# The order of row tiles in the down pairs of a two-layer decoder trunk, and the place of a bias table's product

## The chip, the cores and the metric

The kernel runs on one core of a Trainium2 chip. The metric is the time of one execution in microseconds on the device. Below, TensorE is the matrix engine (PE in the profile), VectorE is DVE, ScalarE is ACT, GpSimd is POOL and SyncE is SP. SyncE only issues transfers here.

## The reference, cut to what matters

The reference is a decoder trunk of two layers for 256 tokens of width 2048. Each layer has a mixer (layer 0: retention and forgetting attention; layer 1: differential attention and a sparse attention with a bias table), a SwiGLU block, and an embedding stage that is gated by the residual stream. The change touches the last matrix product of the SwiGLU block, and, in the embedding stage of layer 0, one small product for the bias table of layer 1.

```python
for i in range(DEPTH):
    ...                                              # mixer: x = x + mix
    h = rmsnorm(x, norm_ffn[i])
    x = x + (jax.nn.silu(h @ ffn_gate[i]) * (h @ ffn_up[i])) @ ffn_down[i]
    x = x + jax.nn.sigmoid(x @ ple_gate[i]) * (p[i] @ ple_proj[i])
return rmsnorm(x, final_norm)
```

The hidden width is 5632. In layer 1 the attention logits get a bias `table[t5_bucket(distance)]` from `t5_table` (32 buckets, 16 heads).

## The kernel before, in words

**Products.** All tokens stand as two halves of 128 rows. An fp32 product is made of three matmuls: each operand is split into a high part (a rounded copy, made by ScalarE) and a low part (the rest, made by VectorE), and high x high, high x low and low x high are summed. A *row tile* is 256 rows by 512 columns of a weight matrix. It is loaded by SyncE into one of five `raw` buffers, split into `whi` and `wlo` (L197, L199), and multiplied with both halves of the tokens: 2 x 2 x 3 = 12 matmuls of 512 columns (L352, L353, L355) into a pair of PSUM accumulators `acc`. There are four of these accumulators, two for each of two blocks of 512 output columns.

**Pairs.** Two blocks of columns, a and b, are computed together as a *pair* (`pair`). For the first 512 rows of the weights the pair uses a scheme of seven products in place of eight, of 6 matmuls each (`Quad`, L421 to L423). They have numbers: 1, 2, 3 and 7 take a weight tile from memory, 5, 6 and 4 take sums of such tiles, which VectorE makes in place (`add`, L385: two sums for product 7, one for 6, one for 4). Sums of the activations (`tabs`) serve as the other operand. After 6 and 5 VectorE combines results in z tiles. The rest of the rows go as plain row tiles, a or b. A string gives the order in which the steps of a pair are taken: a digit is a product, a letter the next row tile of that block. Product 4 completes block a: behind it VectorE adds the parts to both accumulators (`close`, L441, L442) and runs the block's evacuation. Block b is closed and evacuated behind its last row tile.

**The order of issue.** All steps of the program stand in one list, and the kernel is written out by a loop over it (`run`). At each step the splits of weights are issued up to three steps ahead (`LOOK`), then the step's matmuls. Then one tick of `background` passes: small generators (turning a tile, softmax, tables) each issue their next piece when the number of ticks they yielded has passed. Engines work in order, so what is issued first stands first. A weight load is issued when one of the five buffers is free; the tiles of products have their own buffers (`e`, three, and `keys`), and SyncE's queue is in the order of the steps.

**The SwiGLU block.** The 11 blocks of hidden columns are made in three parts: 0 to 3, 4 to 7 and 8 to 10 (here parts 1, 2 and 3; p = 0, 1, 2 in the code). In each part, gate and up of a hidden block form one pair; then the part's hidden blocks are multiplied with `ffn_down` in two pairs, columns 0 and 1, then 2 and 3 (c = 0 and c = 2). A down pair of parts 1 and 2 has 8 row tiles for each block, two of which go into the seven products: 19 steps. One of part 3 has 6, so 15 steps. The last two row tiles of a block read the part's last hidden block, which has just been made: `evac_up` writes it (L1163), and `hid_steps` turns it by way of memory (`turn_far`: two VectorE transposes, L540; one transfer out, L542; four back, L545) and, seven ticks later, splits it into the operand (`split_far`, L498 on ScalarE and L499 on VectorE; the tiles are called Ah, Al or Bh, Bl). Hidden block 10 is turned on TensorE instead (L512). Evacuation of a down block adds it to x (`add_x`, L612); in part 3 it also starts the turn of x for the embedding stage, one column block after the other.

**The embedding stage.** Four row tiles of `ple_proj` come first, one for each block of 512 columns, evacuated by L1195 and L1196, then 32 row tiles of `ple_gate`. At its beginning in layer 0 the generator `toep_steps` starts: it loads the bias table and a one-hot matrix `ohr` by GpSimd (L1028, L1030), yields, multiplies them on TensorE (L1033, a product of 384 columns), copies the result (L1035), writes it to memory spread over 32 rows (L1038) and reads it back in four transfers (L1042) as the table that the attention of layer 1 uses.

Of the kernel before, what the change touches and what calls it, by code (L numbers as in the profile page):

```python
# [95 lines left out]
class Kernel:  # L96
# [344 lines left out]
            tt(blk.acc[0], blk.acc[0], first, op=OP.add)  # L441
            tt(blk.acc[1], blk.acc[1], second, op=op)  # L442

    def pair(self, names, layer, keys, c0, nch, stat, k0, sums, evacs, needs, **kw):

        a, b = (self.Block(self, stat, evac, k0=k0, **{n: v[i] for n, v in kw.items()}) for i, evac in enumerate(evacs))
        q = a.quad = b.quad = self.Quad(self, a, b, stat, k0 + 2 * c0, sums)
        key = {p: (names[i], layer, (keys[i], c0 + c)) for p, i, c in ((1, 0, 0), (2, 0, 1), (3, 1, 1), (7, 1, 0))}
        rest = [(c, c == c0 + nch - 1) for c in range(c0 + 2, c0 + nch)]

        def quad(p):
            self.prog.append(("quad", key.get(p), q, p, needs(c0)))

        def mm(i, c, last):
            self.mm(names[i], layer, (keys[i], c), (a, b)[i], last, needs(c))

        a_rest, b_rest = list(rest), list(rest)
        for what in "1a3a7a6a2aab5b4bbbb" if len(rest) == 6 else "1a3a7a62ab5b4bb":
            if what == "a":
                mm(0, *a_rest.pop(0))  # L460
            elif what == "b":
                mm(1, *b_rest.pop(0))
            else:
                quad(int(what))
# [557 lines left out]
    def toep_steps(self):  # L1022

        nc = self.nc
        self.toep = self.const.tile([P, 16, S], F32, name="tabs")
        tab = self.sc.tile([33, 16], F32, name="tab", bufs=1)
        nc.vector.memset(tab[32:33, :], NEG)
        nc.gpsimd.dma_start(tab[:32, :], self.io["t5_table"])  # L1028
        ohr = self.ring.tile([33, 384], F32, name="z", bufs=8)
        nc.gpsimd.dma_start(ohr, self.io["ohr"])  # L1030
        yield "at", 2
        at = self.ps.tile([P, 512], F32, name="at", bufs=2)
        nc.tensor.matmul(at[:16, :384], tab, ohr, start=True, stop=True)  # L1033
        vec = self.ring.tile([16, 384], F32, name="z", bufs=8)
        nc.scalar.activation(vec, at[:16, :384], AF.Copy)  # L1035

        dv = self.dram.tile([16, 32, 384], F32, name="dv")
        nc.gpsimd.dma_start(dv, vec[:, None].to_broadcast([16, 32, 384]))  # L1038
        yield None, 3
        for q in range(4):  # L1040
            src = bass.AP(tensor=dv.tensor, offset=dv.offset + P - 1 - 32 * q, ap=[[383, 32], [32 * 384, 16], [1, S]])
            nc.gpsimd.dma_start(self.toep[32 * q:32 * q + 32], src)  # L1042
            if q < 3:
                yield None, 1
# [89 lines left out]
    def ffn(self, layer, src, mid, tag, tag2):  # L1134
        K, nc = self, self.nc
        hs = {}

        def evac_gate(blk):
            K.need([("norm", 3)])
            sg = K.zt()  # L1140
            for h in range(2):
                nc.scalar.activation(sg[:, h], blk.acc[h], AF.Silu, scale=K.rstd[:, h:h + 1])
            if blk.j == 10:
                K.table("sigmoid_and_others")
            hs[blk.j] = sg

        def hid_steps(j, k0, hid):
            if j == 10:
                yield from K.turn_fast(hid, mid, k0)
                return  # L1150
            t = K.turn_far(hid)
            yield None, 7
            K.split_far(t, mid, k0)
            if k0 == 0:
                yield None, 1
                for _ in K.sums_of(lambda k, h: K.far(t)[:, k:k + 2, h], K.sums[:, 1]):
                    yield None, 1

        def evac_up(blk):
            sg = hs.pop(blk.j)  # L1160
            hid = K.zt()
            for h in range(2):
                nc.vector.scalar_tensor_tensor(hid[:, h], blk.acc[h], K.rstd[:, h:h + 1], sg[:, h],  # L1163
                                               op0=OP.mult, op1=OP.mult)
            K.spawn(("hid", layer, blk.j), hid_steps(blk.j, (blk.j - blk.j0) * 4, hid),
                    kind="tp" if blk.j == 10 else None)

        def evac_down(blk):
            K.add_x(blk)
            if blk.lastpart:  # L1170
                K.after_x(blk.cb, tag2, src, None, squares=False)

        for p, (j0, j1) in enumerate(FFN_PARTS):
            for j in range(j0, j1):
                if j == 0:
                    self.blocks("ffn_gate", layer, j, 8, src, evac_gate, j=j,
                                needs=[[(tag, c // 2)] for c in range(8)])
                    self.blocks("ffn_up", layer, j, 8, src, evac_up, j=j, j0=j0)
                else:
                    self.pair(("ffn_gate", "ffn_up"), layer, (j, j), 0, 8, src, 0, lambda: K.sums[:, 0],  # L1180
                              (evac_gate, evac_up), lambda c: [("sums", tag)], j=(j, j), j0=(j0, j0))
            for c in range(0, 4, 2):
                if p == 2:
                    self.prog.append(("call", (lambda: K.load_p(layer)) if c == 0 else K.split_p))
                hid = lambda j: [("hid", layer, j // 2)]
                self.pair(("ffn_down", "ffn_down"), layer, (c, c + 1), 2 * j0, 2 * (j1 - j0), mid, -4 * j0,
                          lambda: K.sums[:, 1], (evac_down, evac_down), hid, cb=(c, c + 1), lastpart=(p == 2,) * 2)

    def ple(self, layer, src, tag, tag2, dst, gain):
# [246 lines left out]
```

## Time and profile before

| | us |
|---|---|
| median of 3 runs | 2520.8 |
| lowest and highest run | 2516.07, 2525.46 |
| the profiled execution | 2528.45 |
| its span, from the first to the last instruction | 2526.7 |
| TensorE busy | 2475.3 (98%) |
| VectorE busy | 1860.0 (74%) |
| ScalarE busy | 1291.6 (51%) |
| mean granted clock of TensorE | 0.991 |

Busy time is the union of an engine's instructions in that one execution. The ends of matmuls are modelled: a matmul of 512 columns is shown as 0.39 us, while the next begins 0.23 us after it. A granted clock of 1.00 is TensorE's full speed. Idle time in brackets is that of the engine ahead of the instruction, with what ended it.

### The profile page before, as it was taken

Reading aid. Unit: us, or ns where it says so; the run is one execution under the profiler, and the core shown is the slowest. Engines: PE = TensorE matmul, PEld = TensorE weight load, DVE = VectorE, ACT = ScalarE, POOL = GpSimd, SP = SyncE. Lnnn points to the kernel's source line nnn. Section 1 sums busy time; section 2 is a strip of 40 time slices with the busy share of each in tenths; the row PEclk is TensorE's granted clock in tenths of the full one; section 3 lists DMA queues with packets and bytes.
Section 4 is the critical chain, followed back from the end, with each engine's and each line's share of the span. In section 5 each row is a group of like instructions: output and inputs, shape, how many; then the busy total and the mean of one; then the engine's idle time right before and its main releaser. Section 6 shows DMA issues by size and latency. Waiting matters only on the chain.

```text
span 2526.7 us, 30918 instructions
## 1 busy us (share of the span) xinstructions
PE 2475.3 (98%) x11284; PEld 2034.3 (81%) x11284; DVE 1860.0 (74%) x2427; ACT 1291.6 (51%) x1701; POOL 140.7 (6%) x261
## 2 busy tenths in 40 slices
PE   8999999999999999998999999999999999999998
PEld 7888888787788878776889888878778887888777
DVE  5867756688788887887654666657878888788975
ACT  5444445555445554554553555555544555455554
POOL 0000001000000000101010000010000000000000
PEclk9999999999999999999999999999999999999999
DMA  7655557676556666657857344576665666657564
GB/s 271 188 175 175 184 176 237 205 234 201 189 195 221 224 200 216 206 209 198 254 176 243 129 129 160 172 223 234 200 215 191 208 225 209 215 185 241 176 223 138
DMA packets 146537, 508.70 MB, mean 201 GB/s; under 512 B 18037, under 2 KB 18549, under 8 KB 146256
## 3 DMA queue, kind: packets, MB, share of 16 engines
q1 hardware_dynamic: 132560, 464.25, 55.2%
q0 software_dynamic: 13392, 41.85, 6.1%
q8 instruction: 88, 1.44, 0.2%
q14 instruction: 65, 0.53, 0.1%
q10 hardware_dynamic: 432, 0.62, 0.1%
HBM read 485.42 MB, written 21.23 MB: 201 GB/s over the span
## 4 chain that ended last, share of the span: by engine, by line
PE 77%; DVE 9%; issue 7%; DMA 4%; ACT 2%; POOL 1%; SPq 0%; DVEq 0%; ACTq 0%; POOLq 0%
PE acc L353 22%; PE acc L355 22%; PE acc L352 22%; DVE wlo L199 2%; DVE wlo L182 1%; PE at L422 1%; PE at L421 1%; PE at L423 1%; DMA z<-far 1%; DVE e L385 1%; PE acc L421 1%; PE acc L422 1%; PE acc L423 1%; DMA far<-z 1%; DVE z L1163 1%
## 5 line engine op out<-in xcount | busy, mean ns | idle before, releaser
L199 DVE TENSOR_TENSOR wlo<-raw,whi 128x1024 fp32r<-128x1024 f32 (+3 forms) x753 | 896.6, 1192 | 439.1 <-ACT whi L197 436.9
L197 ACT ACTIVATE whi<-raw 128x1024 fp32r<-128x1024 f32 (+3 forms) x753 | 776.9, 1034 | 554.9 <-PE acc L355 480.3
L352 PE MATMUL acc<-whi,Ah 128*128 128x512 f32 (+1 forms) x1536 | 603.1, 393 | 12.2 <-ACT whi L197 7.3
L353 PE MATMUL acc<-wlo,Ah 128*128 128x512 f32 (+1 forms) x1536 | 598.7, 390 | 5.5 <-DVE wlo L199 4.1
L355 PE MATMUL acc<-whi,Al 128*128 128x512 f32 (+1 forms) x1536 | 596.8, 389 | 2.4 <-DVE Al L499 1.5
L352 PE MATMUL acc<-whi,Bh 128*128 128x512 f32 (+2 forms) x1440 | 560.9, 390 | 4.3 <-ACT Bh L498 4.3
L353 PE MATMUL acc<-wlo,Bh 128*128 128x512 f32 (+2 forms) x1440 | 555.6, 386 | 4.2 <-DVE wlo L199 3.1
L355 PE MATMUL acc<-whi,Bl 128*128 128x512 f32 (+2 forms) x1440 | 554.7, 385 | 1.6 <-DVE Bl L499 1.6
L353 PEld LDWEIGHTS acc<-wlo,Ah 128*128 128x128 f32 x1536 | 291.0, 189 | 73.1 <-DVE wlo L199 16.6
L352 PEld LDWEIGHTS acc<-whi,Ah 128*128 128x128 f32 x1536 | 290.9, 189 | 72.5 <-ACT whi L197 7.3
L355 PEld LDWEIGHTS acc<-whi,Al 128*128 128x128 f32 x1536 | 291.1, 190 | 63.9 <-DVE Al L499 2.9
L353 PEld LDWEIGHTS acc<-wlo,Bh 128*128 128x128 f32 x1440 | 272.3, 189 | 64.9 <-DVE wlo L199 13.9
L352 PEld LDWEIGHTS acc<-whi,Bh 128*128 128x128 f32 x1440 | 271.9, 189 | 57.0 <-ACT Bh L498 5.4
L355 PEld LDWEIGHTS acc<-whi,Bl 128*128 128x128 f32 x1440 | 272.0, 189 | 56.7 <-DVE Bl L499 2.9
L180 ACT ACTIVATE whi<-e 128x1024 fp32r<-128x1024 f32 x160 | 169.7, 1061 | 229.2 <-DVE e L385 154.8
L182 DVE TENSOR_TENSOR wlo<-e,whi 128x1024 fp32r<-128x1024 f32 x160 | 194.6, 1216 | 49.0 <-ACT whi L180 44.9
L385 DVE TENSOR_TENSOR e<-e 128x1024 f32<-128x1024 f32 x96 | 116.9, 1218 | 1.1
L542 POOL DMA_DIRECT2D far<-z x35 | 27.0, 771 | 1446.3 <-DVE z L540 1446.3
L180 ACT ACTIVATE whi<-keys 128x1024 fp32r<-128x1024 f32 x64 | 67.6, 1056 | 54.6 <-DVE keys L385 31.4
L182 DVE TENSOR_TENSOR wlo<-keys,whi 128x1024 fp32r<-128x1024 f32 x64 | 78.3, 1224 | 22.5 <-ACT whi L180 20.9
L545 POOL DMA_DIRECT2D z<-far x140 | 76.6, 554 | 137.9 <-DMA far<-z 59.3
L721 ACT ACTIVATE e<-e,m 128x128 f32<-128x128 f32 (+2 forms) x96 | 40.1, 419 | 75.5 <-DVE m L719 75.5
(298 smaller groups left out, 2186.8 us busy)
## 6 DMA issues: line engine op xcount, KB each, us to landing
raw<-in_ffn_gate SPq DMA_DIRECT2D x136, 512.0 KB, 3.8
raw<-in_ffn_up SPq DMA_DIRECT2D x136, 512.0 KB, 3.5
raw<-in_ffn_down SPq DMA_DIRECT2D x128, 512.0 KB, 3.7
raw<-in_w_in_even SPq DMA_DIRECT2D x103, 512.0 KB, 4.2
raw<-in_w_in_odd SPq DMA_DIRECT2D x80, 512.0 KB, 4.0
raw<-in_ple_gate SPq DMA_DIRECT2D x56, 512.0 KB, 4.5
e<-in_ffn_up SPq DMA_DIRECT2D x40, 512.0 KB, 4.5
e<-in_ffn_down SPq DMA_DIRECT2D x36, 512.0 KB, 4.5
```

Of the source, the lines that this page charges most:

```text
L180: nc.scalar.activation(hi, r, AF.Copy)
L182: nc.vector.tensor_tensor(lo, r, hi.bitcast(F32), op=OP.subtract)
L197: nc.scalar.activation(hi[:, c], r[:, c], AF.Copy)
L199: nc.vector.tensor_tensor(lo[:, c], r[:, c], hi[:, c].bitcast(F32), op=OP.subtract)
L352: nc.tensor.matmul(o, sh, wh, start=not self.started[h], stop=False)
L353: nc.tensor.matmul(o, sh, wl, start=False, stop=False)
L355: nc.tensor.matmul(o, sl, wh, start=False, stop=end)
L385: r, add = self.raw, lambda o, x: self.K.nc.vector.tensor_tensor(o, o, x, op=OP.add)
L421: nc.tensor.matmul(o, sh[:, i], wh, start=start and i == 0, stop=False)
L422: nc.tensor.matmul(o, sh[:, i], wl, start=False, stop=False)
L423: nc.tensor.matmul(o, sl[:, i], wh, start=False, stop=i == 1 and p in (1, 4, 5, 6, 7))
L545: nc.gpsimd.dma_start(back[32 * c:32 * c + 32].rearrange("p (q f) -> p q f", q=4), far[c].rearrange("(q i) f -> i q f", q=4))
```

## The change

Three things change. `pair` takes the order of its steps as an argument, and gate and up get the order that they had. The down pairs get an order for each part and pair:

| part, pair | before | after |
|---|---|---|
| 1 and 2, first | 1a3a7a6a2aab5b4bbbb | 1a3a7a6a2b5bbbaa4bb |
| 1 and 2, second | 1a3a7a6a2aab5b4bbbb | the same |
| 3, first | 1a3a7a62ab5b4bb | 1a3a7b6b2a5a4bb |
| 3, second | 1a3a7a62ab5b4bb | 1a3a7a62a5b4bbb |

And `toep_steps` yields 8 ticks in place of 2 between its two loads and its product. No operation is added or removed.

```diff
-    def pair(self, names, layer, keys, c0, nch, stat, k0, sums, evacs, needs, **kw):
+    def pair(self, plan, names, layer, keys, c0, nch, stat, k0, sums, evacs, needs, **kw):
...
-        for what in "1a3a7a6a2aab5b4bbbb" if len(rest) == 6 else "1a3a7a62ab5b4bb":
+        for what in plan:
...
-        yield "at", 2
+        yield "at", 8
         at = self.ps.tile([P, 512], F32, name="at", bufs=2)
         nc.tensor.matmul(at[:16, :384], tab, ohr, start=True, stop=True)
...
-                    self.pair(("ffn_gate", "ffn_up"), layer, (j, j), 0, 8, src, 0, lambda: K.sums[:, 0],
+                    self.pair("1a3a7a6a2aab5b4bbbb", ("ffn_gate", "ffn_up"), layer, (j, j), 0, 8, src, 0, lambda: K.sums[:, 0],
...
-                self.pair(("ffn_down", "ffn_down"), layer, (c, c + 1), 2 * j0, 2 * (j1 - j0), mid, -4 * j0,
+
+                plan = (("1a3a7b6b2a5a4bb", "1a3a7a62a5b4bbb")[c // 2] if p == 2 else
+                        ("1a3a7a6a2b5bbbaa4bb", "1a3a7a6a2aab5b4bbbb")[c // 2])
+                self.pair(plan, ("ffn_down", "ffn_down"), layer, (c, c + 1), 2 * j0, 2 * (j1 - j0), mid, -4 * j0,
```

## Rows read from the trace of the kernel before

**Rows 1.** the page's first part: busy time, share of the span, instructions

```profile
PE 2475.3 (98%) x11284; PEld 2034.3 (81%) x11284; DVE 1860.0 (74%) x2427; ACT 1291.6 (51%) x1701; POOL 140.7 (6%) x261
```

**Rows 2.** TensorE's waits: who waited for whom, us in total, times, longest

```profile
PE acc L352 <- ACT Ah L498: 4.9, 3, 2.1
...
PE at L1033 <- DMA z<-in_ohr: 4.6, 1, 4.6
PE acc L352 <- ACT Bh L498: 4.3, 3, 2.0
```

**Rows 3.** timeline of TensorE near 634: start, us, instruction, idle before

```profile
633.76 0.39 PE L422 MATMUL acc<-wlo,Bh 128*128 128x512 f32 x1
633.99 0.39 PE L423 MATMUL acc<-whi,Bl 128*128 128x512 f32 x1
...
638.67 0.63 PE L353 MATMUL acc<-wlo,Bh 128*128 128x512 f32 x1
639.10 0.63 PE L355 MATMUL acc<-whi,Bl 128*128 128x512 f32 x1
```

**Rows 4.** windows of TensorE: length, busy (count), granted clock, DMA share, GB/s

```profile
634.38:644.05 9.67, 7.13 (x17) 0.65 0.50 176
898.67:900.90 2.23, 1.06 (x3) 1.00 0.75 231
1880.31:1886.31 6.00, 3.49 (x8) 0.72 0.45 158
2142.92:2149.32 6.40, 4.70 (x12) 0.73 0.56 186
```

**Rows 5.** timeline of ScalarE at the same place

```profile
635.29 1.06 ACT L498 ACTIVATE Bh<-z 128x1024 fp32r<-128x1024 f32 x1 [3.92 <-DMA z<-far]
636.25 1.04 ACT L197 ACTIVATE whi<-raw 128x1024 fp32r<-128x1024 f32 x1
```

**Rows 6.** windows of TensorE at the pair boundary of part 3, both layers

```profile
1136.03:1142.25 6.22, 3.96 (x10) 0.73 0.57 169
2382.33:2388.10 5.77, 3.52 (x8) 0.70 0.57 182
```

**Rows 7.** timeline of VectorE at that boundary, layer 0

```profile
1125.78 0.69 DVE L441 TENSOR_TENSOR acc<-acc,z 128x512 f32<-128x512 f32 x1
...
1129.31 1.29 DVE L540 STREAM_TRANSPOSE z<-x 128x512 f32<-128x512 f32 x2
1130.53 1.18 DVE L182 TENSOR_TENSOR wlo<-e,whi 128x1024 fp32r<-128x1024 f32 x1
...
1134.03 0.67 DVE L499 TENSOR_TENSOR z<-z 128x512 fp32r<-128x512 f32 x1
1134.62 2.47 DVE L385 TENSOR_TENSOR e<-e 128x1024 f32<-128x1024 f32 x2
1137.01 1.22 DVE L199 TENSOR_TENSOR wlo<-raw,whi 128x1024 fp32r<-128x1024 f32 x1
```

**Rows 8.** timeline of VectorE at the pair boundary of part 1, layer 0

```profile
669.28 1.22 DVE L199 TENSOR_TENSOR wlo<-raw,whi 128x1024 fp32r<-128x1024 f32 x1
```

**Rows 9.** the page's sixth part: issues, KB each, us to landing

```profile
e<-in_ffn_down SPq DMA_DIRECT2D x36, 512.0 KB, 4.5
```

**Rows 10.** windows of TensorE at the start of the embedding stage, both layers

```profile
1168.70:1170.76 2.06, 0.30 (x1) 1.00 0.89 239
2415.04:2422.40 7.36, 4.17 (x11) 0.77 0.85 272
```

**Rows 11.** window of VectorE over the second pair of part 3, layer 0

```profile
1145.67:1171.00 25.33, 24.76 (x30) 1.00 0.68 206
```

**Rows 12.** window and timeline of TensorE at the bias table's product

```profile
1178.91:1190.08 11.17, 6.54 (x14) 0.69 0.66 144
...
1183.54 1.43 PE L1033 MATMUL at<-z,tab 33*16 33x384 f32 x2 [4.63 <-DMA z<-in_ohr]
```

## The prediction

> **What bounds the kernel now.** I read the page first: TensorE is busy for 98% of the span [rows 1], so a microsecond is won only where TensorE idles or runs slowly, and a new one is lost only there. Next, the waits of TensorE: apart from the beginning of the program, the large entries are waits for a split of freshly made activations (Ah, Bh) and one wait of 4.6 us for a transfer, in_ohr [rows 2]. Then I went to each of these places with the windows view, to see what a place costs with everything that follows it, and with the timeline, to see the rhythm. At full speed 512-column matmuls start 0.23 us apart [rows 3] (0.2267 over longer stretches), so a row tile of 12 matmuls takes 2.72 us and a product of 6 takes 1.36. After the idle stretch of 2 us at 634 they start 0.43 us apart, at half speed [rows 3]; the window around it has a mean granted clock of 0.65, where 1.00 is 2.4 GHz and 0.50 would be 1.2 [rows 4]. So a stall here costs its idle time and then a row of matmuls at half clock. The cost of a window is its length, plus 0.39 (the modelled duration of the last matmul ahead of it), less 0.2267 for each of its matmuls and one more.
>
> **The row tiles that wait for the last hidden block.** In the first down pair of parts 1 and 2, the step 10 of 19 is the first row tile that reads the hidden block made just before the pair. Four such places (two layers, two parts) stand in rows 4: 9.67 + 0.39 - 18 x 0.2267 = 5.98; 2.23 + 0.39 - 4 x 0.2267 = 1.71; 6.00 + 0.39 - 9 x 0.2267 = 4.35; 6.40 + 0.39 - 13 x 0.2267 = 3.84. Together 15.9 us [rows 4]. In the new order the steps 1 to 9 are the same; then come b, product 5 and three b, which need only older hidden blocks, and the two row tiles stand at steps 15 and 16. That is 4 x 2.72 + 1.36 = 12.2 us later for TensorE, while the longest of the four waits is 2.5 us idle (window less busy) [rows 4]. The whole 15.9 us goes.
>
> What comes late next there: the split of that hidden block is still issued after step 8, since its distance is counted in steps. ScalarE works in order and sits at that split until 635.29; the weight split for step 12 starts behind it, at 636.25 [rows 5]. Its high part is then ready at 637.3 and its low part, which VectorE writes after that of the hidden block, 1.2 us each, at about 638.8. Step 10 would start at 634.22 (0.23 behind the last full-speed matmul, [rows 3]), step 12 at 634.22 + 2.72 + 1.36 = 638.30, and its second matmul wants the low part at 638.53. So 0.3 us is lost where the hidden block lands as late as here, at two of the four places by their window, nothing at the others: -0.6 us. Bounds: nothing, and, if the transfers land 1 us later each, 4 x 1.3 = 5.2.
>
> **Product 4 moves two steps toward the end of the pair.** It completes the first block, so VectorE's four operations that close and add it now come two row tiles ahead of the end instead of four. No row shows this in parts 1 and 2, but the first pair of part 3 ends in the same way already (4, b, b), and its boundary has a stall: 6.22 + 0.39 - 11 x 0.2267 = 4.12 and 5.77 + 0.39 - 9 x 0.2267 = 4.12 [rows 6]. There VectorE has more to do: rows 7 show the first block closed from 1125.78 on, a turn of x for the next stage (1129.31 to 1130.53), a small split after the second block (1134.03 to 1134.62), the two sums of product 7 and only then, at 1137.01, the low part that TensorE waits for. Parts 1 and 2 have neither the turn nor the small split: 1137.01 less 1.22 and 0.59 is 1135.2, the low part is ready 1.2 later, at 1136.4, and TensorE wants it at 1135.86 (the window opens at 1136.03, with the modelled end of the matmul that began at 1135.63). That is 0.55 us late. Today's boundary of part 1 has the low part at 669.28 + 1.22 = 670.50 [rows 8], when it is wanted, and 0.1 to 0.2 us lost. So I take 0.45 more at each of four boundaries, -1.8 us. Bounds: nothing, and 4.12 each (16.5) if the stall is followed by matmuls at half clock as in rows 6. I stay near the low end since no stall of under 1 us here is followed by one: the window at 898 keeps a clock of 1.00 [rows 4].
>
> **The same product on the DMA queue.** SyncE issues weight loads in order, and the next pair's load for product 3 needs the buffer that the sum for product 4 has read; what stands behind it on SyncE are all later weights. The load comes some 5.4 us later against its use; such a load takes 4.5 us [rows 9], and between its issue and its split lie, by the lengths of the steps, 3 x 2.72 + 1.36 + 2.72 = 12.2 us. The pair of part 3 has this distance now, and VectorE's rows at its boundary have no idle ahead of them, so no weight was missing [rows 7]. I cost it at nothing. If the cover were gone, it would be one late load at each of four boundaries.
>
> **Part 3.** In its first pair the products 5 and 4 keep their places and only a and b change order, so the stalls of rows 6 stay; the row tiles that need hidden block 10 go back from step 6 to 10, and the profile shows no wait at that step that could be won. In its second pair 5 and 4 come one step earlier. The first block is closed one row tile earlier, which could shorten the wait at the beginning of the next stage, where the second product of the embedding needs the accumulators of the pair's second block: 2.06 + 0.39 - 2 x 0.2267 = 2.00 and 7.36 + 0.39 - 12 x 0.2267 = 5.03 [rows 10]. But VectorE is busy for 24.76 of the 25.33 us up to there in layer 0 [rows 11], and the same operations stand ahead of that close in either order, so it can start at most 0.6 us sooner. Product 5 one step earlier meets that full queue too and may wait some 0.3 us at the next row tile. I take +0.5 -0.3 in each layer, +0.4 us in all. Bounds: -3 and, if both waits went, +7.
>
> **The bias table's product.** Now TensorE stands from 1178.91 until in_ohr has landed, and the product begins at 1183.54 [rows 12]; the window costs 11.17 + 0.39 - 15 x 0.2267 = 8.16 us, with a granted clock of 0.69. Six steps later are 6 x 2.72 = 16.3 us, and the transfer is missing for 4.63 of them [rows 12]. The product itself stays: 1.43 at the slow clock, about 1 at the full one. So +7.1 us, bounds +6.7 and +7.5. All that the generator does after it moves too, by six steps: a copy on ScalarE, the write of the table and its four reads on POOL's queue. They are needed only by the attention of the next layer. They now share POOL's queue and the DMA engines with the first turn of x out of the embedding stage; that turn's split is seven steps, 19 us, behind its issue, so I cost this at nothing; bound -5, one stall of the size of the middle ones of rows 4.
>
> **The sum.** 15.9 - 0.6 - 1.8 + 0.4 + 7.1 = 21.0 us. The profiled execution took 2528.45 us (span 2526.7); it would take 2507.4. It stands 7.65 above the median of the runs shown, 2520.8, so the median becomes 2499.8. What a measurement of this kernel can tell from no change is about 0.5%, 12.6 us.
>
> **How much of it is the clock.** In the four windows of rows 4 TensorE is busy for 16.39 of 24.30 us, so 7.9 us are idle and the other 8.0 are slow matmuls and restarts; in the window of rows 12 the idle part is 4.6. If only idle time came back, the gain would be 7.9 + 4.6 - 2.4 + 0.4 = 10.5 us and the time 2510. For it speaks that the number of slow matmuls differs from place to place in rows 4; against it, that three of the four windows there and both of rows 6 have them. The Trainium skill ("TensorE: Matmul & The Clock Gate", What's actually happening) advises this reckoning: "For modeling, the ramp penalty is <1% of a typical kernel span; don't fit to a specific cold count." By it the half-clock matmuls would be left out of the sum; the trace agrees that the count varies, but these matmuls are half of what is at stake here.
>
> **The rivals.** First, a pile-up in place of the wait: each of the four boundaries costs 4.12 as in rows 6, and the gain is 15.9 - 0.6 - 16.5 + 0.4 + 7.1 = 6.3 us, 2514.5. It decides from a VectorE delay of 2 us there, where I reckon 0.55. Second, idle time alone comes back, 2510. Third, the table's product does not get out of the way: its later steps push back the turn of x, or the transfer is waited for by another instruction; the gain is 13.9 less up to 5, and the time 2507 to 2512. Fourth, more: both waits of rows 10 go as well, 28 us, 2493. On the other side, loads behind product 4: should the load for product 3 land over 10 us after its issue, where the page has 4.5 [rows 9], SyncE's queue is late at four boundaries by the excess, and the weights behind it too. With 23 us won elsewhere, it makes the kernel slower by 0.5% only from (23 + 12.6) / 4 = 9 us at each, which is a landing time near 20 us: 2534. Nothing in the rows comes near it.
>
> **How the numbers follow.** Forecast 2500: 0.69. Pile-up 2514: 0.11. Idle time alone 2510: 0.06. Table 2507 to 2512: 0.05. More, 2493: 0.06. Loads, 2534: 0.03. The runs of before lie within 4.7 us of their median, and the unknown boundary costs reach a few microseconds further; 2491 to 2512 leaves out most of the pile-up, the loads and a little of the rest, about 2 in 10. Faster by over 0.5%: the forecast, "more" and half of the table case and a little of the rest, 0.80; within: 0.17; slower: 0.03.
>
> **What would show it.** In the profile after: no wait of TensorE at L352 for Ah or Bh in the down pairs, and the clock at 1.00 there; no wait at L1033; a low-part wait of 0.4 to 0.8 us at the fourth step of the second down pair of parts 1 and 2; the stalls of rows 6 as they are. The prediction is wrong if these four boundaries show matmuls at half clock, if step 12 of the first pairs waits over 1 us, or if the embedding stage of layer 0 shows a new wait.

## The result, and the profile after

The changed kernel takes 2508.11 us (median; 2505.35 to 2509.71), the kernel before 2520.94 beside it: a ratio of 0.9947 [0.9931, 0.9963]. The gain is 12.8 us, 0.5%. The time lies 8 us above the forecast of 2500 and inside its range. The profiled execution of after took 2505.35 us (span 2503.6), 2.8 below its median, where that of before stood 7.65 above its own. The two traces so differ by 23.1 us and the medians by 12.8, and a difference between these two traces must not be read as the gain.

In the line numbers of after, everything behind the head of `pair` is one higher, and from the call of the down pairs on four. First the page's busy times and TensorE's waits of after (us in total, times, longest), which answer to [rows 1, 2]:

```profile
PE 2464.2 (98%) x11284; PEld 2025.7 (81%) x11284; DVE 1859.0 (74%) x2427; ACT 1290.1 (52%) x1701; POOL 141.7 (6%) x261
```

```profile
PE acc L353 <- DVE wlo L199: 11.4, 24, 2.3
PE acc L352 <- ACT whi L197: 8.8, 2, 5.7
PE acc L352 <- ACT Bh L499: 1.6, 1, 1.6
PE acc L352 <- ACT Ah L499: 1.6, 1, 1.6
```

The waits for Ah and Bh have gone from three each to one each. The two that are left are at 449 and 1687 us, in the mixers, and before had them too. The wait of 4.6 us for in_ohr has gone. In its place the second row holds two waits for the high part of a weight. The longer one, 5.7, is the first weight of the program, which before waits for too. The other, of 3.0 us, is new.

Windows of TensorE in after: length, busy (count), granted clock, DMA share, GB/s. The first two are the boundaries of parts 1 and 2 in layer 0, the third that of part 3, the fourth is in the embedding stage of layer 0:

```profile
663.19:664.00 0.81, 0.34 (x1) 1.00 0.00 0
922.06:922.86 0.80, 0.33 (x1) 1.00 0.00 0
1127.96:1134.43 6.47, 4.21 (x11) 0.74 0.49 162
1228.60:1236.82 8.22, 4.25 (x10) 0.79 0.42 132
```

By the prediction's reckoning (length + 0.39 - 0.2267 for each matmul and one more) they lose 0.76, 0.75, 4.14 and 6.12 us. The fourth is the new wait. ScalarE around it (start, us, instruction, idle before it and its releaser), then TensorE:

```profile
1218.40 1.06 ACT L197 ACTIVATE whi<-raw 128x1024 fp32r<-128x1024 f32 x1 [0.65 <-DMA raw<-in_ple_gate]
1227.83 1.71 ACT L578 ACTIVATE z<-z,gains 128x256 f32<-128x256 f32 x4 [8.37 <-DMA z<-far]
1229.57 1.06 ACT L499 ACTIVATE Bh<-z 128x1024 fp32r<-128x1024 f32 x1
1230.53 1.04 ACT L197 ACTIVATE whi<-raw 128x1024 fp32r<-128x1024 f32 x1
```

```profile
1228.21 0.39 PE L355 MATMUL acc<-whi,Al 128*128 128x512 f32 x1
1231.62 0.50 PE L352 MATMUL acc<-whi,Ah 128*128 128x512 f32 x1 [3.03 <-ACT whi L197]
```

ScalarE stands for 8.37 us at a turned block of x that has not come back from memory (z<-far). The split of the next weight tile is queued behind it, starts at 1230.53 and is what TensorE, idle for 3.03 us, waits for. Why that block came late is on GpSimd's queue in the same kernel:

```profile
1188.74 0.65 POOL L1039 DMA_DIRECT2D dv<-z  x1 [22.94 <-ACT z L1036]
1198.95 1.97 POOL L1043 DMA_DIRECT2D tabs<-dv  x3 [9.56 <-PE acc L355]
1202.54 0.79 POOL L543 DMA_DIRECT2D far<-z  x1 [1.63 <-DVE z L541]
1218.06 2.33 POOL L546 DMA_DIRECT2D z<-far  x4 [14.73 <-PE acc L355]
1220.38 0.66 POOL L1043 DMA_DIRECT2D tabs<-dv  x1
```

Three of the four reads of the table (tabs<-dv) are issued from 3.6 us ahead of the block's way out (far<-z), and the way back starts only when GpSimd has been idle for 14.73 us behind that. (The releaser named there is not the cause: the instruction wants far<-z landed.) The way out of this one block, from issue to landing:

```profile
DMA to landing us min/median/max: 14.9/14.9/14.9
```

### The profile page after: what moved, and what is told of

Its sections match the earlier page's. It is cut to its first block, busy times and chain, and to the rows that moved or that the text cites. A ratio compares the mean times of both kernels' runs of the same rounds, so it can differ in the third digit from the quotient of the medians.

```text
span 2503.6 us, 30924 instructions
## 1 busy us (share of the span) xinstructions
PE 2464.2 (98%) x11284; PEld 2025.7 (81%) x11284; DVE 1859.0 (74%) x2427; ACT 1290.1 (52%) x1701; POOL 141.7 (6%) x261
## 4 chain that ended last, share of the span: by engine, by line
PE 80%; DVE 12%; issue 4%; DMA 2%; ACT 2%; POOL 0%; SPq 0%; DVEq 0%; ACTq 0%; POOLq 0%
PE acc L353 23%; PE acc L355 22%; PE acc L352 22%; DVE wlo L199 3%; DVE wlo L182 2%; DVE e L385 2%; PE at L422 2%; PE at L421 2%; PE at L423 2%; PE acc L422 1%; PE acc L421 1%; PE acc L423 1%; ACT whi L180 1%; DVE z L1164 1%; DMA z<-far 1%
## 5 line engine op out<-in xcount | busy, mean ns | idle before, releaser
L352 PE MATMUL acc<-whi,Ah 128*128 128x512 f32 (+1 forms) x1536 | 601.0, 391 | 10.6 <-ACT whi L197 8.8
L182 DVE TENSOR_TENSOR wlo<-keys,whi 128x1024 fp32r<-128x1024 f32 x64 | 78.4, 1225 | 17.6 <-ACT whi L180 15.9
```

The lines of the kernel that those rows point to most:

```text
L182: nc.vector.tensor_tensor(lo, r, hi.bitcast(F32), op=OP.subtract)
L352: nc.tensor.matmul(o, sh, wh, start=not self.started[h], stop=False)
```

## The experiments

All times below are medians, and each ratio is against the kernel before in the same batch, with its interval. A diff against "after" is one against the changed kernel.

**before_again.** The kernel before, with no edit, for a second trace and as a measure of the noise.

> The kernel before once more, unchanged, for a second trace and for the spread. Theory A (the trace before was of an execution with longer stalls than most): the four places where the last hidden block is waited for lose less than the 15.9 us of that trace, 8 to 12 us, and the bias table's place less than 8; the median stays at 2521. Rival B (that trace was typical, and the change gives something back that its own trace does not show): again 15 to 16 us at the four places, and a time of this profile near 2528.

2521.59 against 2520.56, 1.0005 [0.9996, 1.0014]. Its profiled execution took 2519.61 us. Windows of TensorE at the four places of [rows 4], then at the table's product of [rows 12]:

```profile
632.73:635.50 2.77, 1.06 (x3) 1.00 0.60 198
893.25:896.08 2.83, 1.06 (x3) 1.00 0.53 193
1874.33:1884.08 9.75, 7.12 (x17) 0.65 0.52 180
2138.70:2141.79 3.09, 1.06 (x3) 1.00 0.49 187
...
1172.49:1184.29 11.80, 6.93 (x15) 0.71 0.63 128
```

The four lose 2.26, 2.33, 6.08 and 2.58 us, 13.3 in all, where [rows 4] gave 15.9; the table's place loses 8.6, no less than the 8.2 of [rows 12]. So neither theory met its figures: the first trace stood high at the four places, but not by as much as theory A has it. Which of the places runs on at half clock changes from one execution to the other: the first had a clock of 0.65 in [rows 4], behind an idle time of 2.02 us, and has 1.00 here, behind 1.18. The waits of [rows 10] lose 2.0 in both layers here, where layer 1 lost 5.03.

**order_only.** The new orders alone, the table's product where it was. Against after:

```diff
-        yield "at", 8
+        yield "at", 2
```

> The new orders of the down pairs alone; the bias table's product stays at 2 ticks. If the order carries the gain and the table's move is nearly paid back by the new wait behind its four reads: 2509 to 2511, with the wait at the table's product back (8 us) and no wait for a turned column block in the embedding stage. If the order only shifts the stalls: 2516 or more.

2503.5 against 2520.56, 0.9928 [0.9915, 0.994]: -17.1 us, by the medians more than both parts together, though the two intervals overlap a little. So the later product seems to cost time here. What I had not foreseen is that the wait at the product became small with the product unmoved. Window of TensorE there, and GpSimd's queue ahead of it:

```profile
1171.90:1174.94 3.04, 1.06 (x3) 1.00 1.01 377
```

```profile
1160.32 0.76 POOL L543 DMA_DIRECT2D far<-z  x1 [10.49 <-DVE z L541]
1164.95 2.19 POOL L546 DMA_DIRECT2D z<-far  x4 [3.87 <-ACT whi L197]
1167.12 0.53 POOL L1029 DMA_DIRECT2D tab<-in_t_table  x1
1167.64 0.55 POOL L1031 DMA_DIRECT2D z<-in_ohr  x1
```

The window loses 2.52 us, not 8.2 to 8.6. The table's two loads stand on GpSimd's queue directly behind the read-back of a block of x that is turned at the end of part 3. When that block comes earlier, so do they.

**table8_only.** The kernel before with the product at 8 ticks.

```diff
-        yield "at", 2
+        yield "at", 8
```

> The move of the bias table's product by six steps alone; the old orders. If its four reads then meet the first turn of x out of the embedding stage and ScalarE stands behind it: the 7 to 8 us at the product go, some 6 come back about 40 us later, and the time is 2518 to 2521. If that new wait belongs to the new orders and not to the move: 2513 to 2514, and no such wait in the trace.

2519.08 against 2520.56, 0.9993 [0.9983, 1.0002]: -1.5 us. The wait at the product is gone (8.2 in [rows 12]); a window of TensorE in the embedding stage has come:

```profile
1232.30:1242.44 10.14, 5.03 (x11) 0.66 0.47 124
```

It loses 10.14 + 0.39 - 12 x 0.2267 = 7.8 us, behind a ScalarE that is idle for 8.55 us until a z<-far has landed at 1232.96. One stall is exchanged for the other, in the old orders as in the new.

**table4.** After, with 4 ticks in place of 8.

```diff
-        yield "at", 8
+        yield "at", 4
```

> The new orders with the bias table's product 2 steps later than before in place of 6 (4 ticks). The in_ohr load landed 1.0 us before the last of the four embedding products ended in the changed kernel, so no wait is left at the product; its four reads are issued four steps, 11 us, earlier than in the changed kernel and are mostly home when the first turn of x begins. Then the wait at 1228 is gone: 2501 to 2503. If the reads meet the turn all the same: 2507 to 2509.

2497.77 against 2520.56, 0.9909 [0.9895, 0.9923]: -22.8 us, faster than after by intervals that do not meet, and faster than the 2501 to 2503 that I expected. TensorE loses 6.1 us at 1228 in after; why the medians differ by 10.3 is open. (The profiled execution, 2501.15, is the slowest of four.) Neither place has a wait of over 1 us. GpSimd's queue:

```profile
1190.67 2.61 POOL L1043 DMA_DIRECT2D tabs<-dv  x4 [9.57 <-PE acc L355]
1205.39 0.79 POOL L543 DMA_DIRECT2D far<-z  x1 [12.11 <-DVE z L541]
1215.16 2.19 POOL L546 DMA_DIRECT2D z<-far  x4 [8.98 <-PE acc L355]
```

The reads stand 14.7 us ahead of the block's way out, the way out lands 9.2 us behind its issue, not 14.9, and the way back waits 8.98 us, not 14.73. ScalarE's wait for the block is 2.25 us, short enough to be hidden.

**reads_late.** After with the product at 8 ticks, but the four reads of the table 40 ticks behind the write, far from the turn of x.

```diff
-        yield None, 3
+        yield None, 40
```

> The changed kernel, with the four reads of the bias table put off by 37 more steps, into the next layer's projection; the table's product, its copy and its write stay where the change put them. If the wait at 1228 of the changed kernel comes from the four reads meeting the first turn of x: it is gone, 2501 to 2503. If it comes from the place of the product or of the write: it stays, 2507 to 2509.

2499.12 against 2521.88, 0.9916 [0.9902, 0.9929]: 9.0 us less than after, the intervals apart. No wait at 1228, which lost 6.1 us in after; and in this trace the boundaries of part 3 lose 2.5 us each, not 4.1, as the last section shows. GpSimd's queue:

```profile
1201.95 0.79 POOL L543 DMA_DIRECT2D far<-z  x1 [13.17 <-DVE z L541]
1208.24 2.21 POOL L546 DMA_DIRECT2D z<-far  x4 [5.50 <-DMA far<-z]
...
1279.39 2.78 POOL L1043 DMA_DIRECT2D tabs<-dv  x4 [0.29 <-issue]
```

With the reads elsewhere and nothing else changed, the same wait is 5.50 us (the way out lands 5.6 us behind its issue). So it is the reads, not the product, the copy or the write, that hold up the turn. Between the block's way out and its way back (1203 to 1218 in after, 1202.7 to 1208.2 here) the DMA engines' busy share is 1.03 in after and 0.95 here, while they move 279 and 334 GB/s: with the reads they are busy throughout and move fewer bytes in a second. This settles the new wait: 5.50 with no reads near, 8.98 with them 14.7 us ahead, 14.73 with three of them 3.6 us ahead.

**parts12_only.** The new first pair of parts 1 and 2 alone; part 3 and the table as before. Against after (and the product at 2 ticks):

```diff
-                plan = (("1a3a7b6b2a5a4bb", "1a3a7a62a5b4bbb")[c // 2] if p == 2 else
+                plan = (("1a3a7a62ab5b4bb", "1a3a7a62ab5b4bb")[c // 2] if p == 2 else
```

> Only the new order of the first down pair of parts 1 and 2; part 3 and the bias table as before. In the traces of the kernel before and of the move alone the four waits for the last hidden block lose 15.9, 13.3 and 10.6 us; the new boundary of the pair costs 0.5 us more at each of four places. If these are what the order is worth there: 2521 less 9 to 13, 2508 to 2512. If part 3 carries the gain: 2516 or more.

2509.86 against 2521.88, 0.9958 [0.9945, 0.997]: -12.0 us. The four waits are gone and each boundary loses 0.76. The four waits lost 15.9, 13.3, 10.6, 16.1 and 13.8 us in the five traces that have the old order (before, before_again, table8_only, part3_second_only, part3_first_only), 13.9 on average. Less 4 x (0.76 - 0.17) = 2.4 for the boundaries, that is 11.5, as measured.

**part3_second_only.** The new second pair of part 3 alone.

```diff
-                plan = (("1a3a7b6b2a5a4bb", "1a3a7a62a5b4bbb")[c // 2] if p == 2 else
-                        ("1a3a7a6a2b5bbbaa4bb", "1a3a7a6a2aab5b4bbbb")[c // 2])
+                plan = (("1a3a7a62ab5b4bb", "1a3a7a62a5b4bbb")[c // 2] if p == 2 else
+                        ("1a3a7a6a2aab5b4bbbb", "1a3a7a6a2aab5b4bbbb")[c // 2])
```

> Only the new order of part 3's second pair (products 5 and 4 one step earlier); all else as before. My prediction gave this 0.4 us. The traces with the new orders show more: the wait at the second embedding product falls from 2.0 to 5.0 us to under 1 in both layers, and the wait at the bias table's product, still 2 ticks behind its loads, from 8 to 2.4, since its loads stand on GpSimd's queue behind the turn that this pair starts. If that is the pair's doing: 6 to 9 us, 2512 to 2515. If it is part 3's first pair or the parts before that do it: 2519 to 2521.

2513.13 against 2521.88, 0.997 [0.996, 0.998]: -8.8 us, for an edit that I had put at +0.4 of gain. Windows of TensorE at the embedding's second product and at the table's product:

```profile
1170.01:1170.84 0.83, 0.34 (x1) 1.00 0.97 336
...
1178.32:1181.05 2.73, 1.06 (x3) 1.00 1.02 393
```

They lose 0.77 us and 2.2 us, the second where it was 8.2 to 8.6. With 0.29 us at its start the embedding's second product loses 1.06 where it lost 2.0, and 0.4 in layer 1. Two low-part waits of 0.34 and 0.46 us, one in each layer, are new next to product 5. That is 0.9 + 1.6 + 6.2 - 0.8 = 7.9.

**part3_first_only.** The new first pair of part 3 alone.

```diff
-                plan = (("1a3a7b6b2a5a4bb", "1a3a7a62a5b4bbb")[c // 2] if p == 2 else
-                        ("1a3a7a6a2b5bbbaa4bb", "1a3a7a6a2aab5b4bbbb")[c // 2])
+                plan = (("1a3a7b6b2a5a4bb", "1a3a7a62ab5b4bb")[c // 2] if p == 2 else
+                        ("1a3a7a6a2aab5b4bbbb", "1a3a7a6a2aab5b4bbbb")[c // 2])
```

> Only the new order of part 3's first pair (a and b change places, products 5 and 4 stay); all else as before. By the prediction it is worth nothing: 2519 to 2523, with the stall of some 4 us at its boundary in place. If it is what is missing between the sum of the other two orders (12.0 and 8.8 us) and the order as a whole (17.1 us), it costs 3 to 4 us: 2524 to 2526.

2519.71 against 2520.96, 0.9999 [0.999, 1.0009]: nothing. By the ratios the three orders give 10.6 + 7.6 + 0.3 = 18.5 us one by one and 18.2 together (order_only), so they add up.

**ends_earlier.** After with 4 ticks, and with product 4 one step further from the end in the first pairs (part 3's first pair gets the order of its second).

```diff
-                plan = (("1a3a7b6b2a5a4bb", "1a3a7a62a5b4bbb")[c // 2] if p == 2 else
-                        ("1a3a7a6a2b5bbbaa4bb", "1a3a7a6a2aab5b4bbbb")[c // 2])
+                plan = (("1a3a7a62a5b4bbb", "1a3a7a62a5b4bbb")[c // 2] if p == 2 else
+                        ("1a3a7a6a2b5bbaa4bbb", "1a3a7a6a2aab5b4bbbb")[c // 2])
```

> The changed kernel with 4 ticks at the bias table, and product 4 one step earlier in two pairs: parts 1 and 2, first: 1a3a7a6a2b5bbaa4bbb; part 3, first: 1a3a7a62a5b4bbb, as its second. If the stalls at the pair boundaries come from the closing of both blocks falling into one burst on VectorE: the 4.1 us at part 3's boundary in both layers fall to under 1.5 each and the 0.8 of parts 1 and 2 to under 0.6; against the 2497.8 of the kernel with 4 ticks some 6 to 8 us less, 2490 to 2492. If the burst is set by the closing of the second block alone, or the products 5 and 4 wait for VectorE instead: 2496 or more.

2495.82 against 2521.88, 0.99 [0.9886, 0.9913]: some 2 us less than table4, which these intervals do not tell apart, where I expected 6 to 8. Windows of TensorE: the boundary of part 3 in both layers, then the embedding's beginning in layer 1:

```profile
1126.52:1127.51 0.99, 0.32 (x1) 1.00 0.17 66
2353.11:2354.12 1.01, 0.33 (x1) 1.00 0.12 45
...
2384.49:2390.41 5.92, 4.43 (x12) 0.71 0.90 307
```

The boundary loses 0.93 and 0.95 us, where it lost 4.12 in [rows 6]: with the two closes further apart the stall is gone, so it was the burst of VectorE's work in [rows 7]. The boundaries of parts 1 and 2 lose 0.18 us each, where after loses 0.76. In this trace 3.4 us are lost anew at the third window, behind a wait of 1.49 us for VectorE's add to x; whether that is why the time fell by so little is not shown.

**ends_earlier_reads_late.** The last one, with the reads of the table late as well.

```diff
-        yield None, 3
+        yield None, 44
```

> The kernel with product 4 earlier in two pairs and 4 ticks at the bias table, with the table's four reads put off into the next layer's projection as well. If the reads cost TensorE nothing any more at 4 ticks: the same 2496, 2494 to 2498. If what is left of their meeting with the first turn of x still costs: 2492 or less.

2492.51 against 2520.96, 0.9888 [0.9872, 0.9903]: -28 us, the lowest median of all, though its interval meets that of ends_earlier, and between the two times that I expected. TensorE keeps a clock of 1.00 at the boundaries and in the embedding stage of layer 0; the wait in the mixer of layer 1 is still followed by half-clock matmuls (3.9 us lost, 2.2 in after).

## Why the prediction was right or wrong, point by point

**Range and direction held, partly by luck: errors cancel.** Against the runs, the term of the hidden block was 2 us too high, that of part 3's second pair 8 too low (+0.4 against 8.8 measured alone), and that of the table's product had the wrong sign beside the new orders (+7.1 against -4.6 by the medians).

**The waits for the last hidden block: right, its size 2 us too high.** They are gone wholly. I took 15.9 us from one execution; five traces give 10.6 to 16.1, 13.9 on average. The idle part is 6.9 to 8.2 us in all of them; what varies more is how many half-clock matmuls follow.

**Step 12: right.** I expected a loss of 0.3 us at two of the four places; after has one of 0.35 at one of them. At the first place ScalarE sits at the split of the hidden block in after too:

```profile
632.91 1.06 ACT L499 ACTIVATE Bh<-z 128x1024 fp32r<-128x1024 f32 x1 [3.02 <-DMA z<-far]
633.88 2.94 ACT L197 ACTIVATE whi<-raw 128x1024 fp32r<-128x1024 f32 x3
```

It waits 3.02 us there, 3.92 in [rows 5], and then makes three weight splits without a pause. TensorE has no wait at that step. In part 1 of layer 1 ScalarE waits for 3.94 us, as long as in [rows 5], and TensorE's second matmul of step 12 comes 0.24 us late (0.35 with the next ones):

```profile
1872.31 0.40 PE L352 MATMUL acc<-whi,Ah 128*128 128x512 f32 x1
1872.78 0.49 PE L353 MATMUL acc<-wlo,Ah 128*128 128x512 f32 x1
```

In reads_late the same step loses 0.76 us.

**The boundary of parts 1 and 2: right.** I put 0.45 us on top of 0.1 to 0.2, a low-part wait with the clock at 1.00; each of the four loses 0.76 at a clock of 1.00 (first fence of windows above). VectorE's timeline at the first one (start, us, instruction) has the three operations that I had counted and neither of the two that make it long in part 3:

```profile
657.60 0.69 DVE L441 TENSOR_TENSOR acc<-acc,z 128x512 f32<-128x512 f32 x1
...
660.00 2.48 DVE L385 TENSOR_TENSOR e<-e 128x1024 f32<-128x1024 f32 x2
662.39 1.22 DVE L199 TENSOR_TENSOR wlo<-raw,whi 128x1024 fp32r<-128x1024 f32 x1
```

So the pile-up did not come, nor did the loads behind product 4: at each of the four, TensorE's wait is for a low part from VectorE, and none is for a transfer.

**Part 3's first pair: right**, at nothing (part3_first_only), its stalls unchanged: 4.1 us in both layers of after (fence of windows above for layer 0).

**Part 3's second pair: the term that was mis-sized.** Predicted +0.4, measured 8.8 [5.0, 10.1 by its ratio's interval]. Two things were missed. The first is the wait of the embedding's second product, 2.0 in each layer (5.03 with the half clock behind it in the first trace), 0.4 in after. I had argued that VectorE's close can start at most 0.6 us sooner. Counted along VectorE's queue from the low part at 1145.67 in [rows 11] (1137.60 in after) it does start 0.55 us sooner, and yet 1.6 us of wait go. TensorE and VectorE in after:

```profile
1160.56 0.39 PE L355 MATMUL acc<-whi,z 128*128 128x512 f32 x1
1160.96 0.50 PE L352 MATMUL acc<-whi,z 128*128 128x512 f32 x1
```

```profile
1159.82 0.69 DVE L441 TENSOR_TENSOR acc<-acc,z 128x512 f32<-128x512 f32 x1
1161.01 1.28 DVE L613 TENSOR_TENSOR x<-acc,x 128x512 f32<-128x512 f32 x2
```

The embedding's second product begins at 1160.96, ahead of VectorE's add of the second block (1161.01), for which it waited before: before_again has TensorE idle for 1.76 and 1.77 us there with that add as releaser. It starts 0.05 us behind the end of ScalarE's evacuation of the first product (1160.31, 0.60 long). That it now takes the accumulators that ScalarE frees is a reading of these rows; the profile does not name the accumulator. The second thing is the table's wait, which I had looked for in the other part of the change. The loads of the table stand behind the read-back of the turned block on GpSimd's queue (order_only), and the earlier close of the first block moves that block, and so them. My step "The first block is closed one row tile earlier" followed this to the next accumulator only, and not along the turn that the same evacuation starts. The 0.3 us that I put on product 5 did come: a low part is late next to it by 0.32 and 0.35 us in the two layers of after.

**The bias table's product: the step that failed.** "That turn's split is seven steps, 19 us, behind its issue, so I cost this at nothing; bound -5." The wait at the product did go (1186.75, with no idle ahead of it), but its reads met the turn of x, the 19 us were not enough, and the window at 1228 lost 6.1 us, a little over my bound. Alone in the old order the move wins 8.2 and pays 7.8 (table8_only, measured -1.5). In the new order the product's wait had come down to 2.5 without it, so the same move pays 6.1 for 2.5; the medians of after and order_only differ by 2508.11 - 2503.5 = 4.6, though their intervals overlap a little; that the reads are dear is shown by table4 and reads_late, whose intervals lie apart from that of after. Most of the +7.1 in my sum was thus won by part 3's second pair already. The prediction named this as the sign of an error ("if the embedding stage of layer 0 shows a new wait"), and gave its third rival, with the time 2507 to 2512, a chance of 0.05. That is the case that came. What the fourth rival named came beside it: both waits of [rows 10] went but for 0.4 us each. So it is the traces, and not the time, that tell the rivals apart.

**The ledger.** Between before_again (2519.61) and after (2505.35), by the matmul starts of both traces: the hidden block +13.3, boundaries of parts 1 and 2 -2.4, embedding waits +3.2, the table's place +1.9 (8.6 to 6.1, and 0.5 at the product itself), part 3's boundaries -1.8 and the wait at 1687 us +1.7 (both by the half clock that follows them or not), product 5 of part 3's second pair -0.7, step 12 -0.4, the program's start -0.2. That is 14.6 us where the two executions differ by 14.3.

**How much of it is the clock.** If idle time alone came back, the four waits would give 7.9 us [rows 4] and, less 2.4, 5.5. parts12_only measured 12.0, with an interval of 7.6 to 13.9. The half-clock matmuls come back too. The Trainium skill ("TensorE: Matmul & The Clock Gate", What's actually happening) puts the ramp penalty at less than 1% of a typical kernel span and advises not to fit a count of cold matmuls. The traces agree with both, since the count varies and 8.0 us is 0.3% of the span. But the gain sought here is of the same size, and leaving those matmuls out would have halved this term.

**What stays open.** What in the reads of the table fills the DMA engines so (their bytes, the shape of their rows, their number, or their place on the queue) was not tried; the profile counts 512 KB for each of the four, as much as for the block's way out. Each would have to be changed by itself. Nor was it tried which accumulator the embedding's second product takes.

## What to carry to other kernels

When a step is moved to get out of a wait, follow each transfer that it issues to the queue it lands on, and ask which round trip is in flight there: the new stall came two engines away, on ScalarE behind a turned block. Follow an operation that ends earlier along everything that its evacuation starts, not only to the next accumulator. And take the size of a stall from several traces: one execution stood 7.65 us from its own median, and the same four waits lost between 10.6 and 16.1 us.

## What the runs showed of the hardware that was not expected

The same idle time has two prices. In before_again TensorE's rows at part 3's boundary, layer 0 and layer 1:

```profile
1133.43 0.51 PE L353 MATMUL acc<-wlo,Bh 128*128 128x512 f32 x1 [2.27 <-DVE wlo L199]
...
2379.16 0.79 PE L353 MATMUL acc<-wlo,Ah 128*128 128x512 f32 x1 [2.27 <-DVE wlo L199]
```

Both follow an idle time of 2.27 us for the same reason, in the same program. The first matmul behind it takes 0.51 us in one and 0.79 in the other, and the places lose 2.6 and 4.0 us. In reads_late both layers keep the full 2.4 GHz at this place, and in after neither does (0.74 in the third window of after above, and 0.74 in layer 1):

```profile
1128.32:1130.90 2.58, 0.33 (x1) 1.00 0.70 203
2357.04:2359.62 2.58, 0.32 (x1) 1.00 0.61 200
```

They lose 2.5 us each. Shorter stalls do the same. These follow 1.18 us of idle time, and 0.53 more two matmuls later, at the fourth place of [rows 4] and at the first of before_again:

```profile
2144.09 0.50 PE L352 MATMUL acc<-whi,Ah 128*128 128x512 f32 x1 [1.18 <-ACT Ah L498]
...
633.91 0.50 PE L352 MATMUL acc<-whi,Bh 128*128 128x512 f32 x1 [1.18 <-ACT Bh L498]
```

The windows there have a clock of 0.73 and of 1.00, and lose 3.84 and 2.26 us. I found nothing in the rows ahead of a stall that tells which it will be. So a stall of some 2.3 us at part 3's boundary is worth 2.5 to 4.2 us, and no single one of these.
